# The gate projection as a Strassen-Winograd product: three of its seven quarter products between the attention's matmuls, four in a stage behind the pooling projection

## The chip, the cores and the metric

The kernel runs on one core of a Trainium2 chip. The metric is device time in microseconds (us) of one execution, from the first to the last instruction with what the launch adds around it; of the kernel before, three executions are given, and one more was taken with a profile.

## The reference, cut to what matters

One residual layer on 1024 tokens with 1024 channels, in fp32. What the change touches is the line with `gates`; what stands around it decides where that work may be placed.

```
h = rmsnorm(x, g_mix)
z = h @ w_in                       # pooling | q | k | v columns
y_pool = pool_mixer(u_pool, w_pool_grp, pool_scale)
y_attn = diff_attention(q, k, v, g_q, g_k, lam, g_sub)     # 8 heads
gates  = sigmoid(h @ w_gate + b_gate)                      # 1024 x 2048
merged = gates[:, :1024] * (y_pool @ w_branch_pool)
       + gates[:, 1024:] * (y_attn @ w_branch_attn)
x = x + merged @ w_out
x = x + square(relu(rmsnorm(x, g_ffn) @ w_up)) @ w_down
```

The matrix h enters as its transpose hT (channels by tokens), and so every gate block is 128 gate columns by 1024 tokens.

## The kernel before, in words

**Arithmetic.** Every fp32 operand of a matmul is split into a high part (a cast, made by ScalarE) and a low part (source minus high part, made by VectorE or GpSimd; `split`, L115). A product is then three matmuls into one PSUM bank, high by high, high by low, low by high (`mm3`, L120; its three calls are L123, L124 and L125, and after the change L122, L123 and L124). "A matmul of 512 columns" below is one of those three.

**Stages.** First come the norm of x and its transpose into hT (8 tiles of four 128-channel blocks each in high and low parts). Then the attention: 8 heads with 8 query tiles each, a software pipeline whose stages run one or more tiles apart (`stage_qkv` makes z for tile t, `stage_prep` norms it, `stage_qkT` transposes q and k (tk), `stage_scores` (sc), `stage_aT` transposes the weights (ta), `stage_pv` (po), `stage_norm`). Names such as z5_6 mean head 5, tile 6. z has two PSUM banks, sc two, the transposes (tk, ta) two, po one, and one bank is left for the fillers (`ps_f`, tag "f").

**Fillers.** Two kinds of independent matmuls are written behind the attention in the program, and so have a lower priority: the pooling mixer (u, 24 matmuls for each of 8 pieces, and yp, 3 each) and the gate projection (`gate_cols`, L744: 16 column blocks, each 2 halves of 24 matmuls, named g0 to g15; the result plus bias goes through a two-buffer pool "fo" to the DRAM tensor `g_dram`). The order on each engine is fixed when the program is built: a list scheduler takes, at each step, the instruction of highest priority whose inputs it expects to be ready. A filler therefore stands wherever it expected TensorE to have nothing of the attention to do; what is left of them runs behind the attention. Each engine, and each queue of transfers (SyncE's "SP" and ScalarE's), works strictly in the order given.

**Behind the attention.** The pooling projection bp (`branch_pool`, L218; 16 groups of 12 matmuls; the result stays in SBUF as mp), then the attention's projection ba (16 groups of 24), multiplied by the gates that are read back from `g_dram` (`gate`, L207, which applies the sigmoid), then the output projection op, then the MLP. The MLP's two projections are already Strassen-Winograd products before the change.

**Scheme.** With hT and w_gate cut in halves each way (channels by tokens, gate columns by channels), the 2 by 2 block product needs 8 quarter products the plain way, and 7 by Winograd's form of Strassen's scheme with sums of quarters as operands. For each of 8 column blocks d (128 columns of the first and the same 128 of the second gate half), one quarter product is 4 blocks of k by three matmuls: 12 matmuls of 512 columns.

Of the kernel before, what the change touches and what calls it, by code (L numbers as in the profile page):

```python
# [17 lines left out]
P = 128  # L18
S = 1024
# [18 lines left out]
N_QKVW = 8 * H  # L38
# [11 lines left out]
G_FIRST, G_Z = 13, 13  # L50
# [5 lines left out]
def encoder_kernel(  # L56
# [63 lines left out]
    def mm3(ps, lhs_hi, lhs_lo, rhs_hi, rhs_lo, first, last, more=False):  # L120

        kw = {"skip_group_check": True} if more else {}  # L122
        nc.tensor.matmul(ps, lhs_hi, rhs_hi, start=first, stop=False, **kw)  # L123
        nc.tensor.matmul(ps, lhs_hi, rhs_lo, start=False, stop=False, **kw)  # L124
        nc.tensor.matmul(ps, lhs_lo, rhs_hi, start=False, stop=last, **kw)  # L125

    wcount = [0]

    def wt(shape, name, dt=F32R):

        wcount[0] += 1
        if wcount[0] > N_QKVW and (wcount[0] - N_QKVW - 1) % (N_W + N_FW) >= N_W:
            return fw_tile(shape, name, dt)
# [73 lines left out]
    def gate(gts, c):  # L207
        for gt, c0, c1 in gts:
            nc.sync.dma_start(gt, g_dram[c * P : (c + 1) * P, c0:c1])
            nc.scalar.activation(gt, gt, AF.Sigmoid, bias=zero)  # L210

    def whole(g):
        return [(g, 0, S)], [g[:, 0:512], g[:, 512:S]]
# [3 lines left out]

    def branch_pool(d, ws, ps_fn):  # L218

        m = htile([P, S], F32, f"mp{d}", 1)  # L220
        for th in range(2):
            ps = proj_T(ps_fn(f"bp{d}_{th}"), ws, lambda k, th: pair(ypT[k][th]), th, nk=4)
            nc.scalar.copy(m[:, th * 512 : (th + 1) * 512], ps)
        mp.append(m)
# [14 lines left out]
    zero = const.tile([P, 1], F32, name="zero")  # L239
    y_dram = dram.tile([D, S], F32, name="y_dram")  # L240
# [48 lines left out]
    with ExitStack() as ph:  # L289
# [119 lines left out]
        gghs = {}  # L409
# [19 lines left out]
        def stage_qkv(h, t):  # L429
# [4 lines left out]
            for k in range(NK):  # L434
# [3 lines left out]
                mm3(z[:, 0:384], l_hi, l_lo, w[:, 0, :], w[:, 1, :], k == 0, k == NK - 1)  # L438
# [47 lines left out]
        def stage_scores(h, t):  # L486
# [44 lines left out]
            if (h, t) == (H - 1, NT - 1):  # L531

                nc.vector.tensor_scalar(zero, Z[:, 1, t : t + 1], 0.0, None, op0=ALU.mult)
            st[h, t]["a"] = s[0]
# [209 lines left out]
    def gate_cols(c):  # L744
        ws = fill_w(w_gate, c * P, f"gate{c}")
        for th in range(2):
            ps = fill_proj(ws, th, f"g{c}_{th}", spare_bank if c >= G_Z else fill_bank)
            fo = fo_tile(f"go{c}_{th}")
            nc.scalar.activation(fo[:, 0:512], ps, AF.Identity, bias=cols[:, c : c + 1])  # L749
            nc.scalar.dma_start(g_dram[c * P : (c + 1) * P, th * 512 : (th + 1) * 512], fo[:, 0:512])  # L750
            yield

    def gates():
        for c in range(2 * NK - 2):
            yield from gate_cols(c)
        for gen in [gate_cols(c) for c in (2 * NK - 2, 2 * NK - 1)] * 2:
            next(gen)
            yield

    gate_units = gates()  # L760
    for _ in range(G_FIRST):
        next(gate_units)
    for g in range(4):
        for _ in pool_group(g):
            next(gate_units)
    for _ in gate_units:
        pass
# [16 lines left out]
    def ypt_tile(shape, dt, name, th):  # L784
        return htile(shape, dt, name, 0)
# [10 lines left out]


    ws_bp = {0: load_cols2(w_branch_pool, 0, "bp0")}
    ypT = [load_split(p_dram, g * P, f"ypT{g}", ypt_tile) for g in range(4)]
    mp, yT, ws_ba = [], [], {}  # L800

    for d in range(NK):
        if d % 2 == 0 and d + 2 < NK:
            ws_bp[d + 2] = load_cols2(w_branch_pool, (d + 2) * P, f"bp{d + 2}")
        elif d > NK - 4:
            j = len(ws_ba)
            ws_ba[j] = load_cols(w_branch_attn, j * P, f"ba{j}")
        branch_pool(d, ws_bp[d - d % 2][d % 2], bank)
        if d % 4 < 2:
            rb = [fu_tile(f"rb{d}") if d % 2 else ut([P, S], F32, f"rb{d}")]  # L810
        else:
            rb = [tmp(f"rb{d}_{i}") for i in range(2)]
        yT.append(load_split(y_dram, d * P, f"yT{d}", yt_tile(d), (rb, r_dram[d])))
    mT = {}
    for d in range(NK):
# [3 lines left out]
        gp = [tmp(f"gp{d}_{th}") for th in range(2)]  # L819
        gate([(gp[0], 0, 512), (gp[1], 512, S)], d)  # L820
        for th in range(2):
# [506 lines left out]
```

## Time and profile before

| | us |
|---|---|
| three executions | 1574.85, 1574.85, 1577.69 |
| median | 1574.85 |
| the profiled execution: its time / its span | 1577.1 / 1575.3 |
| busy in the span: TensorE matmul / VectorE / ScalarE / GpSimd | 1549.7 / 936.4 / 814.5 / 356.0 |

The span runs from the first to the last instruction; 1.8 us of the profiled execution's time lie around it. The busy time of TensorE overstates its work, since a matmul of 512 columns is shown with 0.39 us while the next one starts 0.23 us after it; so it is the starts, or the number of matmuls in a stretch, that tell how dense TensorE is. By the rows' times, attention runs from about 25 us to 629 us (its last z at 576), the rest of the fillers to 722, bp to 765, ba to 855, op and the second norm to about 950, and the MLP to the end.

### The profile page before, as it was taken

The page shows a single profiled execution, that of the slowest core. Times are in us where ns is not written, and L with a number is a line of the kernel's source. Part 1 is how long each engine was busy: PE and PEld are TensorE (multiplying, and loading weights), DVE is VectorE, ACT ScalarE, POOL GpSimd, SP SyncE. Part 2 cuts the span into 40 slices and gives each one's busy share as a digit, 9 for nine tenths or more (in the row PEclk, how much of TensorE's full clock was granted, in tenths as well). Part 3 has the DMA queues.
Part 4 walks back from the last instruction along what each step waited for, and adds up shares of the span by engine and source line. Part 5 has one row for each costly group of instructions (what it writes and reads, how often), then busy time and mean ns, then how long its engine had stood idle before and what let it go on. Part 6 is the DMA issues. An engine that isn't in the chain of part 4 may idle for free.

```text
span 1575.3 us, 21905 instructions
## 1 busy us (share of the span) xinstructions
PE 1549.7 (98%) x7713; PEld 1328.0 (84%) x7713; DVE 936.4 (59%) x1925; ACT 814.5 (52%) x1810; POOL 356.0 (23%) x456
## 2 busy tenths in 40 slices
PE   7999999999999999899999999999999999999999
PEld 6999999999999997688888887888888788888887
DVE  6766666666676766206442358866655667546562
ACT  6656575765656665225542547555555633333331
POOL 5424252433434332313454400000000000000000
PEclk9999999999999999999999999999999999999999
DMA  7102020201112112229547533554342799437650
GB/s 226 56 29 75 28 71 26 69 29 55 58 36 64 45 53 76 91 100 309 159 128 219 172 114 122 185 185 157 128 140 107 274 345 355 161 121 253 221 186 27
DMA packets 168008, 206.94 MB, mean 131 GB/s; under 512 B 10117, under 2 KB 104026, under 8 KB 167898
## 3 DMA queue, kind: packets, MB, share of 16 engines
q1 hardware_dynamic: 150490, 178.23, 34.8%
q10 hardware_dynamic: 17408, 27.30, 4.7%
q8 instruction: 61, 1.00, 0.3%
q14 instruction: 49, 0.40, 0.1%
HBM read 150.94 MB, written 54.56 MB: 130 GB/s over the span
## 4 chain that ended last, share of the span: by engine, by line
PE 91%; DMA 3%; ACT 2%; DVE 2%; issue 1%; SPq 0%; POOL 0%; ACTq 0%; DVEq 0%; POOLq 0%
PE z L125 5%; PE z L123 5%; PE z L124 5%; PE Da L124 4%; PE Da L123 4%; PE g L123 4%; PE Da L125 4%; PE g L124 4%; PE g L125 4%; PE Db L124 3%; PE Db L123 3%; PE Db L125 3%; PE X L125 2%; PE X L123 2%; PE X L124 2%; PE sc L508 2%
## 5 line engine op out<-in xcount | busy, mean ns | idle before, releaser
L125 PE MATMUL z<-wqkv,hT 128*128 128x384 f32 x512 | 174.6, 341 | 0.3 <-DVE hT L118 0.2
L123 PE MATMUL z<-wqkv,hT 128*128 128x384 f32 x512 | 174.6, 342 | 0.1
L124 PE MATMUL z<-wqkv,hT 128*128 128x384 f32 x512 | 174.0, 340 | 0.0
L519 ACT ACTIVATE s<-s,nm 128x256 f32<-128x256 f32 (+7 forms) x128 | 99.7, 779 | 57.7 <-DVE nm L511 56.2
L123 PE MATMUL g<-hT,fwgate 128*128 128x512 f32 x256 | 101.7, 398 | 4.5 <-ACT go L749 2.4
L449 POOL TENSOR_TENSOR ms<-ms,mhalf 128x4 f32<-128x4 f32 x64 | 70.7, 1104 | 156.0 <-DVE ms L447 153.2
L124 PE MATMUL g<-hT,fwgate 128*128 128x512 f32 x256 | 101.6, 397 | 0.0
L125 PE MATMUL g<-hT,fwgate 128*128 128x512 f32 x256 | 100.8, 395 | 0.0
L123 PEld LDWEIGHTS z<-wqkv,hT 128*128 128x128 f32 x512 | 96.9, 189 | 3.7 <-ACT hT L117 0.7
L125 PEld LDWEIGHTS z<-wqkv,hT 128*128 128x128 f32 x512 | 96.8, 189 | 3.1 <-DVE hT L118 1.4
L124 PEld LDWEIGHTS z<-wqkv,hT 128*128 128x128 f32 x512 | 96.9, 189 | 2.9
L511 DVE CUSTOM_DVE_ANT_0 s<-sc,dist 128x512 f32<-128x512 f32 (+3 forms) x128 | 74.9, 587 | 23.0 <-PE sc L509 21.5
L508 PE MATMUL sc<-K,Q 128*128 128x512 f32 (+2 forms) x192 | 69.0, 362 | 0.7 <-DVE nm L511 0.5
L509 PE MATMUL sc<-K,Q 128*128 128x512 f32 (+2 forms) x192 | 66.5, 355 | 0.0
L118 DVE TENSOR_TENSOR AS<-s,AS 128x512 fp32r<-128x512 f32 x64 | 43.9, 690 | 35.4 <-ACT AS L117 35.2
L118 POOL TENSOR_TENSOR wqkv<-rqkv,wqkv 128x384 fp32r<-128x384 f32 x60 | 62.4, 1058 | 7.9 <-ACT wqkv L117 6.7
L123 PEld LDWEIGHTS g<-hT,fwgate 128*128 128x128 f32 x256 | 48.4, 189 | 15.3 <-ACT go L749 3.9
L118 POOL TENSOR_TENSOR fwgate<-frgate,fwgate 128x512 fp32r<-128x512 f32 x32 | 42.9, 1343 | 72.0 <-ACT fwgate L117 72.0
L125 PEld LDWEIGHTS g<-hT,fwgate 128*128 128x128 f32 x256 | 48.5, 190 | 9.0
L458 POOL TENSOR_TENSOR qn<-qn,ggh 128x128 f32<-128x128 f32 x64 | 30.1, 470 | 115.0 <-DVE qn L452 101.9
L479 DVE TENSOR_TENSOR K<-tk,K 64x128 fp32r<-64x128 f32 x128 | 36.9, 288 | 31.9 <-ACT K L478 28.2
L124 PEld LDWEIGHTS g<-hT,fwgate 128*128 128x128 f32 x256 | 48.5, 189 | 8.1
(424 smaller groups left out, 4548.8 us busy)
## 6 DMA issues: line engine op xcount, KB each, us to landing
wd<-in_w_down_dram SPq DMA_DIRECT2D x56, 512.0 KB, 5.2
wu<-in_w_up_dram SPq DMA_DIRECT2D x32, 512.0 KB, 5.5
udS<-us SPq DMA_DIRECT2D x64, 256.0 KB, 2.4
ur<-udS SPq DMA_DIRECT2D x32, 512.0 KB, 4.8
rqkv<-in_w_in_dram SPq DMA_DIRECT2D x64, 192.0 KB, 2.8
ud<-u ACTq DMA_DIRECT2D x48, 256.0 KB, 2.5
ur<-ud SPq DMA_DIRECT2D x24, 512.0 KB, 3.8
frgate<-in_w_gate_dram SPq DMA_DIRECT2D x32, 256.0 KB, 2.7
```

The source lines that it names most:

```text
L118: return (lo_eng or nc.vector).tensor_tensor(lo, src, f(hi), op=ALU.subtract)
L123: nc.tensor.matmul(ps, lhs_hi, rhs_hi, start=first, stop=False, **kw)
L124: nc.tensor.matmul(ps, lhs_hi, rhs_lo, start=False, stop=False, **kw)
L125: nc.tensor.matmul(ps, lhs_lo, rhs_hi, start=False, stop=last, **kw)
L449: nc.gpsimd.tensor_tensor(ms, ms, mhalf[:, 0:4], op=ALU.pow)
L458: nc.gpsimd.tensor_tensor(qn[:, 2:4, :], qn[:, 2:4, :], ggh.unsqueeze(1).broadcast_to([P, 2, HD]), op=ALU.mult)
L479: nc.vector.tensor_tensor(K[other, m, c0 : c0 + P], k, f(k_hi), op=ALU.subtract)
L508: nc.tensor.matmul(dst, Q[:, i, 0, :], rhs, start=True, stop=False)
L509: nc.tensor.matmul(dst, Q[:, i, 1, :], rhs, start=False, stop=True)
L511: nc.vector.tensor_tensor_reduce(out=s[i][:, c : c + w], in0=sc[:, 0:w], in1=dist[:, o0 + c : o0 + c + w], scale=2.0 ** -(h + 1), scalar=B ...
L519: nc.scalar.activation(s[i][:, 0:n], s[i][:, 0:n], AF.Exp, bias=last, scale=-1.0, accum_out=Z[:, i, t : t + 1])
```

## The change

The 16 plain column blocks (8 by 2 by 2 by 24, 768 matmuls of 512 columns) are replaced by 8 blocks d of 7 quarter products (672 matmuls).

- **As fillers** (`gate_first`): products A11*B11 and A12*B21 into one bank (gA), and S4*B22 into another (gB). After the first product ScalarE copies the bank out (x1, to the new DRAM tensor `xz`), and the second product accumulates onto it, which gives the finished quarter C11. The operand S4 = A11 + A12 - A21 - A22 is made on GpSimd from four loads of a weight quarter; these loads share a pool of two buffers ("fr"). `G_TAIL = 5`: only the blocks 0 to 2 are free to go anywhere; 3 to 7 are held back with `issue_after` until the third-last z of the last head.
- **In a stage of their own** (`gate_rest`), behind the pooling projection: first the quarters of hT are replaced in place by T2, T1, T3 and T4 (16 additions and subtractions of 128x1024, ten on VectorE and six on GpSimd, and 8 splits), then for each d the four products with S2, S1, S3, A22. VectorE splits these operands and adds the PSUM results to x1 and z3 read back from `xz`; finished quarters go to `g_dram`.
- The loads and the splitting of the attention's result (`load_yT`) move from the pooling projection into this stage. The pooling projection's result goes out to DRAM (`mp_dram`) and comes back in ba. The gate's bias is added in the sigmoid (`gbias`).

```diff
-G_FIRST, G_Z = 13, 13
+G_FIRST, G_Z, G_TAIL = 4, 3, 5
...
-            nc.scalar.activation(gt, gt, AF.Sigmoid, bias=zero)
+            nc.scalar.activation(gt, gt, AF.Sigmoid, bias=gbias[:, c : c + 1])
...
+    def gate_first(d):
+        rows_d = slice(d * P, (d + 1) * P)
+        r11, r12 = gate_raw(11, d), gate_raw(12, d)
+        w11, w12 = gate_split(r11, f"A11_{d}"), gate_split(r12, f"A12_{d}")
+        ps = spare_bank(f"gA{d}") if d >= G_Z else fill_bank(f"gA{d}")
+        mm_quarter(ps, w11, 0, 0, True, True)
+        keep(ps, xz[rows_d, 0, :], f"x1_{d}")
+        nc.gpsimd.tensor_tensor(r12, r11, r12, op=ALU.add)
+        mm_quarter(ps, w12, 2, 0, False, True, True)
+        keep(ps, g_dram[rows_d, 0:512], f"C11_{d}")
+        for q in (21, 22):
+            nc.gpsimd.tensor_tensor(r12, r12, gate_raw(q, d), op=ALU.subtract)
+        w4 = gate_split(r12, f"S4_{d}")
+        yield
+        ps = spare_bank(f"gB{d}") if d >= G_Z else fill_bank(f"gB{d}")
+        mm_quarter(ps, w4, 2, 1, True, True)
+        keep(ps, xz[rows_d, 1, :], f"z3_{d}")
+        yield
...
+    early, late = units[: 2 * (NK - G_TAIL)], units[2 * (NK - G_TAIL) :]
...
+    with tc.issue_after(z_last[H - 1, NT - 1 - 2].ins):
+        for gen in late:
+            next(gen)
...
+    for kp in range(2):
+        a, b, c, e = (fw_tile([P, 2, 512], f"comb{n}{kp}", F32) for n in "abce")
...
+        add(dve, a, f(B12[0]), f(B12[1]))
+        add(pool, b, f(B22[0]), f(B22[1]))
+        add(pool, e, f(B21[0]), f(B21[1]))
+        sub(dve, c, b, a)
+        sub(dve, a, a, f(B11[0]))
+        sub(dve, a, a, f(B11[1]))
+        sub(dve, b, b, a)
+        sub(pool, e, e, b)
+        for room, t in ((B11, b), (B12, a), (B22, c), (B21, e)):
+            split(*room, t)
...
+        for name, rw in (("S2", r11), ("S1", s1), ("S3", r21), ("A22", r22)):
+            w = wt([P, 2, 4, P], f"{name}_{d}")
+            split_made[d] = split(w[:, 0], w[:, 1], rw)
...
+        A = bank(f"gA_{d}")
+        gate_mm(A, ws[0], 2, True, True)
+        add(dve, u[:, 0, :], A, v[:, 0, :])
```

Two places where the order of instructions moves. The first is TensorE in head 5, at the end of z5_5. Before the change, gate matmuls (g6_1) stand between the scores of the tile (sc5_1):

```order
L125 MATMUL z5_5_4639<-wqkv5_7_3987,hT3_1_1_339 128x384
L123 MATMUL g6_1_7174<-hT0_1_0_332,fwgate6_0_7087 128x512
L124 MATMUL g6_1_7174<-hT0_1_1_333,fwgate6_0_7087 128x512
L125 MATMUL g6_1_7174<-hT0_1_0_332,fwgate6_0_7087 128x512
L509 MATMUL sc5_1_0_0_4526<-K5_0_4156,Q2_238 128x256
L123 MATMUL g6_1_7174<-hT0_1_0_332,fwgate6_0_7087 128x512
```

After it, at the same place on TensorE, the rows are those of the attention alone:

```order
L124 MATMUL z5_5_4640<-wqkv5_7_3988,hT3_1_1_340 128x384
L491 MATMUL sc5_1_0_0_4527<-K5_0_4157,Q2_239 128x256
L548 MATMUL ta4_7_0_4455<-identf_90,s4_7_0_4330 128x128 x4
L492 MATMUL sc5_1_0_0_4527<-K5_0_4157,Q2_239 128x256
L491 MATMUL sc5_1_1_0_4550<-K5_0_4157,Q2_239 128x256
L548 MATMUL ta4_7_1_4475<-identf_90,s4_7_0_4330 128x128 x4
```

In the changed order no filler stands between the last yp behind z4_5 and the first gA4 behind z7_5, which is 24 tiles (z4_6 to z7_5); before, there were 11 to 26 fillers at the tiles 0, 1 and 5 of these heads.

The second place is GpSimd in the drain of the attention, between qn7_7 (the normed q and k of the last tile) and the memsets of the last two weight tiles (AT7_2, AT7_3). Before the change:

```order
L458 TENSOR_TENSOR qn7_7_6425<-qn7_7_6425,ggh7_5720 128x128
L118 TENSOR_TENSOR wgrp2_7469<-rgrp2_7467,wgrp2_7469 128x128
L551 MEMSET AT7_2_4_6450 128x128 x2
L722 COPY sum2_0_1_7499<-u2_7472 128x1
L722 COPY sum2_0_2_7502<-sum2_0_1_7499 128x2
L722 COPY sum2_0_4_7505<-sum2_0_2_7502 128x4
```

After it the operands of the held-back blocks stand there (A11_5 and A12_5 are splits of loaded quarters, ga12_5 the sum that becomes S4_5):

```order
L117 TENSOR_TENSOR S4_4_7436<-ga12_4_7390,S4_4_7436 128x512
L441 TENSOR_TENSOR qn7_7_6426<-qn7_7_6426,ggh7_5721 128x128
L117 TENSOR_TENSOR A11_5_7459<-ga11_5_7455,A11_5_7459 128x512
L117 TENSOR_TENSOR A12_5_7462<-ga12_5_7457,A12_5_7462 128x512
L765 TENSOR_TENSOR ga12_5_7457<-ga11_5_7455,ga12_5_7457 128x512
L535 MEMSET AT7_2_4_6451 128x128 x2
L769 TENSOR_TENSOR ga12_5_7457<-ga12_5_7457,ga21_5_7497 128x512
L769 TENSOR_TENSOR ga12_5_7457<-ga12_5_7457,ga22_5_7500 128x512
L117 TENSOR_TENSOR S4_5_7503<-ga12_5_7457,S4_5_7503 128x512
```

The chain of these operands is now in one queue with the attention's own small operations.

More of the change, by code (lines that the diff above doesn't have):

```diff
@@ L753, in gates, with gate_raw @@
[L753 to L760, printed above, removed]
+    xz = dram.tile([D, 2, 512], F32, name="xz")
+    def gate_raw(q, d):
+        r0, c0 = (q % 10 - 1) * 512, (q // 10 - 1) * D + d * P
+        rw = fr_tile([P, 4, P], f"ga{q}_{d}")
+        nc.sync.dma_start(rw, w_gate[r0 : r0 + 512, c0 : c0 + P].rearrange("(kk p) c -> p kk c", p=P))
+        return rw
@@ L802, in encoder_kernel @@
+    gens = [gate_rest(d) for d in range(NK)]
     for d in range(NK):
```

170 lines of the change are left out of this document (119 added, 51 removed).

## The prediction

> **What bounds the kernel now.** I read the page first (busy shares, the chain that ended last), then TensorE by windows, then its starts where the windows thin out.
>
> ```profile
> PE 1549.7 (98%) x7713; PEld 1328.0 (84%) x7713; DVE 936.4 (59%) x1925; ACT 814.5 (52%) x1810; POOL 356.0 (23%) x456
> ...
> PE 91%; DMA 3%; ACT 2%; DVE 2%; issue 1%; SPq 0%; POOL 0%; ACTq 0%; DVEq 0%; POOLq 0%
> ```
>
> The chain of waits is TensorE for 91%, so a matmul less is time less, as long as nothing else becomes late. The price of one is not its 0.39 us but the distance between starts. A window inside ba, where only matmuls of 512 columns run (time, TensorE busy and count, clock, share of the transfer engines, GB/s):
>
> ```profile
> 775.00:800.00 25.00, 25.00 (x108) 1.00 0.46 149
> ```
>
> 25 / 108 = **0.2315 us** each. In the attention the same view gives, for 480 us, all engines (TensorE, weight loads, VectorE, ScalarE, GpSimd), then TensorE alone for z, g, u and yp in this order:
>
> ```profile
> 80.00:560.00 480.00, 479.46 (x2893) 449.63 (x2892) 322.69 (x977) 300.06 (x890) 180.22 (x251) 1.00 0.16 48
> 80.00:560.00 480.00, 264.55 (x1277) 1.00 0.16 48
> 80.00:560.00 480.00, 87.51 (x326) 1.00 0.16 48
> 80.00:560.00 480.00, 25.62 (x96) 1.00 0.16 48
> 80.00:560.00 480.00, 2.85 (x9) 1.00 0.16 48
> ```
>
> 1277 / 24 = 53.2 tiles, 9.02 us each. The 431 fillers cost 431 x 0.2315 = 99.8 us of that; the attention by itself asks TensorE for (480 - 99.8) / 53.2 = **7.15 us** a tile. TensorE never stands still here, but it is full because there are fillers, which is the point on which this prediction turns.
>
> **The change part by part.** *Fewer matmuls.* 768 become 672: 96 x 0.2315 = **-22.2 us**. The order of the changed program on TensorE has 672 rows of gA and gB where 768 of g stood, so the change does what it says.
>
> *The thin stretch behind the attention goes.* All engines, then the starts at one place in it:
>
> ```profile
> 629.40:722.00 92.60, 86.19 (x366) 68.56 (x365) 17.30 (x27) 27.20 (x46) 27.36 (x26) 0.98 0.37 121
> ```
>
> ```profile
> 650.62 0.39 PE L125 MATMUL g<-hT,fwgate 128*128 128x512 f32 x1
> 651.84 0.50 PE L123 MATMUL yp<-mix,wgrp 128*128 128x512 f32 x1 [0.83 <-ACT go L749]
> ...
> 654.48 0.63 PE L125 MATMUL g<-hT,fwgate 128*128 128x512 f32 x1
> 654.91 0.63 PE L123 MATMUL g<-hT,fwgate 128*128 128x512 f32 x1
> ```
>
> 366 matmuls ask for 84.7 us and took 92.6: 7.9 us are lost, because the fillers of one bank wait for ScalarE to empty it. In the changed order these fillers are gone from here, and bp with 8 banks follows the attention: **-7.9 us**. What is late next is the drain of the attention, below.
>
> *The heads without fillers.* In 24 tiles no filler is left. If TensorE stays the bound, a tile takes 7.15 us; if the other engines need the 9.02 us that they have now, the fillers were free and nothing is won: the bounds are 0 and 24 x 1.87 = +44.9 us against the sum. In between lies what VectorE needs of its own, 322.7 / 53.2 = 6.07 us a tile, and the waits in which ScalarE has to act first and that no faster TensorE removes, in the same window (busy, mean ns, then the idle time before them and its releaser):
>
> ```profile
> L479 DVE TENSOR_TENSOR K<-tk,K 64x128 fp32r<-64x128 f32 x105 | 30.3, 289 | 29.1 <-ACT K L478 26.4
> L481 DVE TENSOR_TENSOR Q<-tk,Q 64x128 fp32r<-64x128 f32 x104 | 29.8, 286 | 13.9 <-ACT Q L480 12.0
> L118 DVE TENSOR_TENSOR AT_0l<-ta,AT_0h 128x512 fp32r<-128x512 f32 x35 | 24.2, 690 | 15.0 <-ACT AT_0h L117 14.0 <-ACT oq L588 0.7
> ...
> L526 DVE RECIPROCAL cf<-Z 128x1 f32<-128x1 f32 x54 | 8.8, 162 | 27.4 <-ACT s L519 27.0
> ```
>
> 26.4 + 12.0 + 14.0 + 27.0 = 79.4 us, 1.49 a tile. 6.07 + 1.49 = 7.56 us: just above TensorE's 7.15. I take 7.56, **+9.8 us** (24 x 0.41), since it is the only value that rests on waits and not on an extreme.
>
> *The drain of the attention.* The five held-back blocks start behind z7_5 (557.7 in the trace). The stretch from there to the last po, all engines, then g, u and yp:
>
> ```profile
> 557.70:629.40 71.70, 69.83 (x390) 60.10 (x389) 46.58 (x127) 41.15 (x115) 19.39 (x29) 1.00 0.21 66
> 557.70:629.40 71.70, 18.83 (x72) 1.00 0.21 66
> 557.70:629.40 71.70, 18.29 (x72) 1.00 0.21 66
> 557.70:629.40 71.70, 2.66 (x9) 1.00 0.21 66
> ```
>
> Without its 153 fillers (35.4 us) the drain is 36.3 us; with 180 new ones 78.0, which the sum of matmuls contains. But their operands come one after another through two load buffers. The steps, from the nearest rows: a cast, a low part, an addition, a load.
>
> ```profile
> L117 ACT CAST fwgate<-frgate 128x512 fp32r<-128x512 f32 x12 | 7.4, 619 | 20.8 <-PE g L125 17.5 <-PE u L125 3.1 <-DMA frgate<-in_w_gate_dram 0.2
> ```
>
> ```profile
> L831 POOL TENSOR_TENSOR mg<-mg,mp 128x512 f32<-128x512 f32 x16 | 21.5, 1343 | 25.2 <-DVE mg L830 25.2
> L118 POOL TENSOR_TENSOR fwgate<-frgate,fwgate 128x512 fp32r<-128x512 f32 x14 | 18.3, 1310 | 47.9 <-ACT fwgate L117 47.9
> ```
>
> ```profile
> frgate<-in_w_gate_dram SPq DMA_DIRECT2D x32, 256.0 KB, 2.7
> ```
>
> One block: 3 additions (4.03), 3 loads in line (8.1), 2 casts (1.24), 2 low parts (2.62) = 16.0 us. Four such rounds are 64 us of a stretch of 78, so 14 us remain for queueing: what waits behind these steps is GpSimd's own memsets and qn7_7, and behind gB6 and gA7 on TensorE the last ta and po. At best nothing is lost. At worst each of the 10 steps finds one other GpSimd instruction ahead (180.22 / 251 = 0.72 us in the attention): 7.2 us a round, 28.7 in all, of which 15 stick out. I take a value near the low end, since the 14 us of room come first: **+4 us**.
>
> *The stage of its own.* Per block TensorE has 48 matmuls, 11.1 us. VectorE has 4 low parts, 2 scalings and 2 low parts for yT, 4 additions from PSUM. Their rows, and transfers beside bp today:
>
> ```profile
> L823 DVE TENSOR_TENSOR mp<-mp,gp 128x512 f32<-128x512 f32 x16 | 16.2, 1022 | 21.3 <-ACT gp L210 21.1
> L118 DVE TENSOR_TENSOR yT<-ryT,yT 128x512 fp32r<-128x512 f32 x16 | 14.8, 971 | 3.9 <-ACT yT L117 3.9
> ...
> L830 DVE TENSOR_TENSOR mg<-ba,ga 128x512 f32<-128x512 f32 x16 | 10.9, 684 | 0.4 <-PE ba L125 0.4
> ```
>
> ```profile
> 722.00:765.00 43.00, 43.00 (x191) 35.53 (x190) 27.75 (x28) 27.56 (x49) 19.11 (x14) 1.00 0.83 271
> ```
>
> At 0.684 throughout, 12 operations are 8.2 us; with 0.97 for the eight that read SBUF twice, 10.5. Both fit under 11.1. GpSimd's four additions are 5.4 us. The loads and stores are about 3 MB a block, 276 GB/s: what bp bears today (271 GB/s at 0.83) with TensorE full. Bounds: nothing, and, if VectorE and GpSimd could never overlap, 8.2 + 5.4 - 11.1 = 2.5 us a block, +20 us. I take a quarter of it, as the 10.5 still leave 0.6 us a block: **+5 us**.
>
> The shorter VectorE durations belong to operations from PSUM, the longer to those with two SBUF inputs beside a busy GpSimd. The Trainium skill, "SBUF — State Buffer", section "Who interferes with whom", calls this an exclusive lock: one of the two engines blocks for the whole instruction. The rows agree in direction (1.02 against 0.68); by the rule taken strictly the stage would cost the +20 and not the +5, the third rival.
>
> *At nothing:* rebuilding hT. An operation of 1024 columns on VectorE:
>
> ```profile
> L118 DVE TENSOR_TENSOR u_0l<-ur,u_0h 128x1024 fp32r<-128x1024 f32 x1 | 1.2, 1227 | 0.4 <-ACT u_0h L117 0.4
> ```
>
> 18 of them are 22 us, and GpSimd's six, at twice 1.343, 16; both lie beside bp's 192 matmuls (44 us), and without that cover they are +22. The pooling result's way through DRAM costs two stores per 5.6 us and one load per 11.1 in stages whose transfers have room (0.46 in ba).
>
> **Sum:** -22.2 - 7.9 + 9.8 + 4 + 5 = -11.3. The profiled execution took 1577.1, so 1565.8; the median lies 2.25 below it: **1563.5 us**.
>
> **The rivals.**
> - *Nothing waits:* -30.1, 1545. For it: in all 480 us TensorE shows no wait, so every other engine keeps up with it today. Against it: VectorE's 7.56, and two queues with a chain of loads behind z7_5.
> - *The fillers were free:* the heads keep up to 9.02 us a tile, since they stand just where the scheduler saw a gap. At 9.02 the sum is +23.8, 1599. It decides from 7.56 + 11.3 / 24 = 8.03 us a tile; from there the change is slower. For it: VectorE and ScalarE together have 622.8 us of work in 480, so they seldom rest at once. Against it: each is idle for a third of the time, and VectorE's 7.56.
> - *VectorE and GpSimd exclude each other* in the new stage: +20 for +5, 1578.5.
> - *The slow clock.* Behind two waits of 1 us, at 651 and 653, the granted clock fell to half:
>
> ```profile
> 654.00:656.00 2.00, 2.00 (x6) 1.55 (x5) 0.00 (x0) 0.00 (x0) 0.00 (x0) 0.50 0.38 139
> ```
>
> Eight matmuls at 0.43 in place of 0.23 lost 1.6 us. If every place where a block of fillers stood in these tiles (about five a head, 14 in all) does this, +22: 1586. The Trainium skill, "TensorE: Matmul & The Clock Gate", Part 1, wants an idle window of about 3.4 us for it; by that, holes of 1 us would cost nothing, and the trace here shows that two of them sufficed.
>
> **How the numbers follow.** Forecast 0.52 (1552 to 1572), nothing waits 0.12, free fillers 0.18, exclusion 0.12, clock 0.06. The range reaches from 1547, just above the first rival, to 1586 with the clock, and leaves out the worst of the second. A difference of 0.2%, 3.1 us, is about what a measurement of this kernel can tell. Faster by more: forecast 0.50 and first rival, 0.62; within: edges of the forecast and of the exclusion, 0.11; slower: free fillers, half of the exclusion, most of the clock, 0.27.
>
> **What will show it.** Tiles z4_6 to z7_5 at 7.6 us (7.15 and 9.0 are the rivals); no window with waits on ScalarE for a bank behind the attention; fewer than 5 us of TensorE waiting at gB6, gA7, gB7 for S4 and A12; in the new stage about 108 matmuls per 25 us. Wrong would be a longer attention, or a stage in which TensorE waits for VectorE's low parts.

## The result, and the profile after

The changed kernel takes **1611.83 us** (median of 4 executions, 1610.63 to 1616.73), the kernel before beside it 1576.27 (4 executions, 1574.85 to 1579.47). The ratio is 1.0229, with a 95% interval of 1.0201 to 1.0256: 2.3% slower, where 1563.5 us was forecast. The profiled execution is the longest of the four (1616.7 us, its span 1614.9), so the sums below, made between the two profiled executions (1577.1 and 1616.7), explain +39.6 us, four more than the medians differ.

The page of the changed kernel:

```profile
PE 1558.2 (96%) x7617; PEld 1324.0 (82%) x7617; DVE 1019.7 (63%) x2004; ACT 820.1 (51%) x1824; POOL 443.6 (27%) x508
...
PE 41%; DMA 2%; DVE 1%; ACT 0%; issue 0%; POOL 0%; SPq 0%; ACTq 0%; DVEq 0%
```

TensorE executes 96 matmuls less and is busy 8.5 us longer. The second line is cut short by what the profile could follow back; that TensorE has 41% where it had 91% is no measure of waiting. For that the work is cut into the same four stages in both kernels: first z to last z, from there to the end of bp (with the thin stretch or the drain's fillers), then to the first op, then the rest. Windows before (columns: length, then busy time and count of TensorE, weight loads, VectorE, ScalarE and GpSimd, granted clock, share of the transfer engines, GB/s), and after:

```profile
11.00:575.60 564.60, 563.62 (x3370) 527.02 (x3371) 383.79 (x1158) 360.07 (x1072) 225.62 (x310) 1.00 0.18 57
575.60:761.50 185.90, 177.61 (x817) 144.51 (x816) 79.36 (x141) 82.22 (x164) 56.72 (x56) 0.99 0.43 140
761.50:851.10 89.60, 89.60 (x385) 72.09 (x385) 34.36 (x44) 36.83 (x57) 45.79 (x34) 1.00 0.46 145
851.10:1575.30 724.20, 716.89 (x3137) 582.73 (x3135) 436.26 (x578) 331.51 (x510) 23.02 (x23) 1.00 0.54 184
```

```profile
10.80:571.80 561.00, 543.61 (x3200) 503.40 (x3200) 396.47 (x1176) 352.85 (x1068) 245.84 (x334) 0.98 0.19 60
571.80:690.40 118.60, 108.49 (x509) 87.48 (x507) 75.51 (x113) 59.58 (x129) 69.45 (x48) 0.97 0.50 162
690.40:888.20 197.80, 185.61 (x769) 148.20 (x770) 106.80 (x131) 69.64 (x106) 95.42 (x67) 0.96 0.61 198
888.20:1614.90 726.70, 718.69 (x3137) 583.32 (x3135) 438.21 (x581) 334.11 (x515) 28.14 (x27) 1.00 0.55 185
```

From each stretch its matmuls of 512 columns are taken off at 0.2315 us. Up to the last z these are 503 fillers before and 336 after; then 481 fillers and 192 of bp before, 168 and 192 after; then 384 of ba before, and 384 of the four products and 384 of ba after. What is left is the attention's own work, and waiting:

| stretch | before | after | difference | the prediction's terms |
|---|---|---|---|---|
| first z to last z | 564.6 - 116.4 = 448.2 | 561.0 - 77.8 = 483.2 | **+35.0** | +9.8 |
| to the end of bp | 185.9 - 155.8 = 30.1 | 118.6 - 83.3 = 35.3 | **+5.2** | -7.9 + 4 |
| own stage and ba | 89.6 - 88.9 = 0.7 | 197.8 - 177.8 = 20.0 | **+19.3** | +5 |
| start, op and MLP | | | +2.3 | 0 |
| 96 matmuls fewer | | | -22.2 | -22.2 |
| sum | | | **+39.6** | -11.3 |

So the saving came as forecast, and 61.8 us were lost around it. The attention has 167 fillers less (38.7 us) and became 3.6 us shorter. The clock column shows a second thing. It falls to 0.5 for 3.4 us at a time, in ten places, 40.9 us together; before it did so once. Three of them:

```profile
44.60:48.00 3.40, 3.40 (x10) 2.62 (x9) 1.31 (x5) 1.25 (x4) 2.88 (x3) 0.50 0.21 80
362.00:365.40 3.40, 3.40 (x16) 3.19 (x15) 2.63 (x9) 1.65 (x7) 1.01 (x1) 0.50 0.41 145
713.60:720.40 6.80, 5.71 (x13) 4.46 (x14) 6.80 (x8) 1.10 (x3) 3.69 (x3) 0.50 0.34 110
```

Three holes in front of TensorE, each with the rows that lead to it (start, us, engine, line, operation, in brackets the idle time before and its releaser). At the start, GpSimd's `rs` of a token norm stands behind an addition for S4 that waited for its load, and VectorE's `hn` waits for `rs`:

```profile
38.56 1.29 POOL L769 TENSOR_TENSOR ga<-ga,ga 128x512 f32<-128x512 f32 x1 [1.54 <-DMA ga<-in_w_gate_dram]
39.81 0.55 POOL L232 TENSOR_TENSOR rs<-rs,mhalf 128x1 f32<-128x1 f32 x1
40.39 2.42 DVE L253 SCALAR_TENSOR_TENSOR hn<-x,rs,gmb 128x512 f32<-128x512 f32 x2 [1.29 <-POOL rs L232]
43.29 0.63 PE L258 MATMUL hps<-identf,hn 128*128 128x128 f32 x4 [2.94 <-DVE hT L117]
```

In the new stage, the sum s1 waits 8.2 us for a buffer that a store of bp's result still holds (both go through "fo"), and S2 is made from s1. Its cast also stands on ScalarE behind a copy of bp's result (mp) that waits 5.6 us for the same buffers; both waits end within 0.2 us of each other:

```profile
697.87 1.29 POOL L821 TENSOR_TENSOR s<-gr 128x512 f32<-128x512 f32 x1 [8.22 <-DMA mp_dram<-mp]
701.45 0.59 ACT L755 COPY mp<-bp 128x512 f32<-128x512 f32 x1 [5.56 <-DMA mp_dram<-mp]
702.43 0.62 ACT L116 CAST S<-ga 128x512 fp32r<-128x512 f32 x1 [0.40 <-ACT mp L755]
703.10 0.61 PE L122 MATMUL gA<-hT,S 128*128 128x512 f32 x1 [4.02 <-ACT S L116]
```

And in bp, a copy that would free a PSUM bank stands on ScalarE behind a cast that waits 4.5 us for a load:

```profile
647.60 1.14 ACT L116 CAST wbp<-rbp 128x512 fp32r<-128x512 f32 x2 [4.45 <-DMA rbp<-in_w_branch_pool_dram]
648.64 0.58 ACT L755 COPY z<-gB 128x512 f32<-128x512 f32 x1
649.27 0.79 PE L122 MATMUL bp<-ypT,wbp 128*128 128x512 f32 x1 [3.20 <-ACT z L755]
```

### The profile page after: what moved, and what is told of

The parts are those of the page before. It is cut to its first block, busy times and chain, and to the rows that moved or that the text cites. A ratio compares the mean times of both kernels' runs of the same rounds, so it can differ in the third digit from the quotient of the medians.

```text
span 1614.9 us, 21978 instructions
## 1 busy us (share of the span) xinstructions
PE 1558.2 (96%) x7617; PEld 1324.0 (82%) x7617; DVE 1019.7 (63%) x2004; ACT 820.1 (51%) x1824; POOL 443.6 (27%) x508
## 5 line engine op out<-in xcount | busy, mean ns | idle before, releaser
L548 PE MATMUL ta<-identf,s 128*128 128x128 f32 x288 | 48.2, 277 | 7.0 <-DVE s L511 3.4
L465 ACT CAST Q<-tk 64x128 fp32r<-64x128 f32 x128 | 33.2, 260 | 39.6 <-DVE Q L464 37.0
L122 PE MATMUL op<-wo,mT 128*128 128x512 f32 x128 | 50.2, 395 | 1.8 <-ACT wo L116 1.8
L463 ACT CAST Q<-tk 64x128 fp32r<-64x128 f32 x128 | 33.0, 258 | 36.7 <-DVE K L462 35.4
L124 PE MATMUL ba<-yT,wba 128*128 128x512 f32 x128 | 50.5, 395 | 0.0
L122 PE MATMUL ba<-yT,wba 128*128 128x512 f32 x128 | 50.5, 395 | 0.0
L123 PE MATMUL ba<-yT,wba 128*128 128x512 f32 x128 | 50.5, 395 | 0.0
```

Source lines behind the costliest of these rows:

```text
L124: return nc.tensor.matmul(ps, lhs_lo, rhs_hi, start=False, stop=last, **kw)
L465: nc.scalar.copy(Q[other, m, 1, :], q)
L548: nc.tensor.transpose(ta[:, i * P : (i + 1) * P], a[:, (4 * j + i) * P : (4 * j + i + 1) * P], identf)
```

## The experiments

The theory from these rows: the loss has two parts, the place of the work (the attention lacks fillers) and single instructions that stand in an engine's strict queue behind something that waits; both make holes, and holes bring the half clock. The times of single executions vary by 2 to 5 us, so differences below that are read from traces.

**e1: no block held back.**

```diff
-G_FIRST, G_Z, G_TAIL = 4, 3, 5
+G_FIRST, G_Z, G_TAIL = 4, 8, 0
```

> The changed kernel, but none of the eight blocks of first products is held back (G_TAIL 0, all of them in the fillers' bank). By its order on TensorE all 504 fillers then stand between z0_0 and z6_5: heads 5 and 6 get 150 and head 7 and the drain none, where the changed kernel has none in heads 5 to 7 and 168 in the drain. Theory 1 (without fillers a tile needs 8.1 us because its own steps wait for one another, with fillers 9.0): heads 5 and 6 go from 65 to about 72 us each, head 7 stays near 63, and the drain falls from 68 us to about 48, since 39 us of matmuls leave it and not all of its holes can close; 1600 to 1610 us in all. Rival (a tile without fillers is TensorE's 7.15 us, and what the changed kernel lost there was the half clock behind its holes): heads 5 and 6 at 75 us, head 7 at 58 us, drain 37 us, about 1590.

Measured 1612.2 us (one execution), 2 us above theory 1's range. With 78 and 72 fillers the heads 5 and 6 took 75.0 and 80.5 us, where theory 1 had 72 for each and the rival 75; head 7 without any took 63.3, as theory 1 had it, and the drain without any 57.3 us, nine more than the theory gave it. The drain's window:

```profile
594.90:652.20 57.30, 40.03 (x178) 28.82 (x176) 47.00 (x103) 32.83 (x81) 10.34 (x12) 0.73 0.21 68
```

A clock of 0.73 over 57 us: 30.7 us of it ran at half. The rival's 1590 is out, though its 75 us was right for head 5, and the theory had the drain too cheap. The lack of fillers only moved from heads 5 and 6 to head 7 and the drain.

**e3: the old products in the new places.** Plain blocks, two of them free and 14 held back:

```diff
-    for _ in range(G_FIRST):
+    for _ in range(4):
         next(gate_units)
     for g in range(4):
         for _ in pool_group(g):
-            next(gate_units)
-    for _ in gate_units:
-        pass
+            pass
+    with tc.issue_after(z_last[H - 1, NT - 1 - 2].ins):
+        for _ in gate_units:
+            pass
```

> The kernel before with its plain gate blocks, but only two of them are free fillers beside the pooling mixer; the other 14 are held back until the third-last z, as the change holds its five blocks. In its order the heads 5 to 7 have 13 fillers instead of 205. No Strassen product in the gates at all: this is the place of the work alone. Theory 1 (fillers cost a tile 0.9 us where they fill 2.06): heads 5 to 7 at 8.1 us a tile, 65 us each instead of 73, and the time rises by about 180 x 0.2315 less some 20, with the thin one-bank stretch longer: +20 to +38 us, 1597 to 1615. Rival (TensorE bound, 7.15 to 7.56 us a tile): 0 to +12, 1577 to 1589.

Measured 1592.9 us, **+16.2** against 1576.7 beside it, with no Strassen product in the gates at all. It lies between the two expectations, and so does the tile: head 6, with no filler, took 60.7 us, 7.59 a tile, not 8.1. Heads 5 (13 fillers) and 6:

```profile
362.90:426.80 63.90, 62.71 (x384) 58.10 (x383) 49.39 (x148) 41.74 (x131) 25.94 (x37) 1.00 0.15 46
426.80:487.50 60.70, 59.04 (x371) 55.53 (x370) 45.96 (x145) 40.41 (x131) 23.19 (x36) 1.00 0.12 36
```

The same heads of the changed kernel, both with no filler, at 8.21 and 8.07 us a tile and a clock of 0.97:

```profile
378.70:444.40 65.70, 61.39 (x372) 56.96 (x371) 45.77 (x146) 40.60 (x131) 24.24 (x39) 0.97 0.11 33
444.40:508.90 64.50, 61.03 (x370) 57.05 (x369) 46.15 (x146) 41.26 (x131) 22.47 (x35) 0.97 0.14 42
```

Each of these heads has one stretch of half clock, at most 1.7 us of its time or 0.2 a tile. The attention's own time per tile, head duration less fillers at 0.2315 us, over 8:

| head | 0 | 1 | 2 | 3 | 4 | 5 | 6 | 7 |
|---|---|---|---|---|---|---|---|---|
| before | 6.16 | 7.08 | 7.21 | 7.12 | 7.11 | 7.12 | 7.11 | 7.12 |
| changed | 6.82 | 7.08 | 7.14 | 7.32 | 8.25 | 8.21 | 8.07 | 7.52 |
| e3, plain, held back | 6.13 | 7.08 | 7.36 | 7.26 | 7.54 | 7.60 | 7.59 | 7.47 |
| e6 (below) | 6.99 | 7.08 | 7.14 | 7.32 | 8.16 | 7.96 | 7.60 | 7.42 |
| e12, mixed (below) | 6.24 | 7.13 | 7.18 | 7.18 | 7.21 | 7.18 | 7.27 | 7.11 |

Of the 35.0 us, some 16 go with the place alone (e3's whole row is 16.0 above before's). It may be more, since e3 still has 51 fillers in heads 5 to 7 and the changed kernel 12.

The price of a filler can be read here too. Head 6 of the kernel before, with 68 fillers:

```profile
430.70:503.40 72.70, 72.70 (x438) 68.23 (x437) 49.67 (x152) 45.41 (x138) 27.04 (x39) 1.00 0.15 47
```

72.7 less e3's 60.7 is 12.0 us for 68 fillers, 0.18 each, both at full clock.

**e4: fillers that do nothing.**

```diff
+    wd = gate_split(gate_raw(11, 0), "wd")
+    for i in range(14):
+        mm_quarter(fill_bank(f"dm{i}"), wd, 0, 0, True, True)
```

> The changed kernel with 168 more fillers that nobody reads (14 groups of 12 matmuls of 512 columns on a first weight quarter), which by the order fall into heads 4 to 7: 69, 60 and 39 in heads 5, 6 and 7. It does extra work and leaves nothing out. At full price they are 38.9 us. Theory 1 (other engines' steps set the pace of a tile without fillers): a tile goes from 8.1 to 9.0 us, half the price or less, +10 to +20 us; the half-clock stretches in the heads go. Rival (a tile is TensorE's 7.15 and the rest is the half clock): the fillers cost their full price less the clock's 2 to 4 us, +35. Third (fillers are entirely free): within 4 us of the changed kernel's 1612.

Measured 1625.3 us, +13.5 against the changed kernel's median. Heads 5 and 6:

```profile
376.60:449.60 73.00, 73.00 (x440) 68.41 (x440) 46.13 (x144) 42.13 (x130) 22.53 (x35) 1.00 0.09 27
449.60:520.60 71.00, 71.00 (x431) 66.64 (x430) 46.65 (x144) 42.04 (x129) 23.42 (x36) 1.00 0.13 39
```

69 and 60 fillers lengthened them by 7.3 and 6.5 us: **0.11 us for a filler that costs 0.2315 elsewhere**. The clock is at 1.00 and TensorE without a gap again; part of the low price is the half clock that went with the fillers' return, at most 1.7 us a head. Less its fillers at full price, head 5 is back at 7.13 us a tile, where the kernel before has 7.12. Theory 1 holds; neither "full price" nor "free".

**e2: buffers of its own for bp's result.**

```diff
+        mo = ut([P, S], F32, f"mo{d}")
...
-            keep(ps, mp_dram[d * P : (d + 1) * P, hs], f"mp{d}_{th}")
+            nc.scalar.copy(mo[:, hs], ps)
+            nc.scalar.dma_start(mp_dram[d * P : (d + 1) * P, hs], mo[:, hs])
```

> The changed kernel, but the pooling projection's result goes to DRAM through buffers of its own (three of the class U, a whole row block each) instead of the two buffers fo, which the operand sum s1 of the last four products also uses. Theory 1 (the own stage starts late because s1 of blocks 0 and 1 waits behind stores of the pooling projection for a buffer fo): the waits of gA for ScalarE's casts at 699 and 710 us and the half clock behind them go, -6 to -12 us, 1600 to 1606. Rival (VectorE and GpSimd block one another there, and the operands come late for that): the work of both is the same, so no more than -2 us.

Measured 1602.5 us, -9.4. From the end of bp to op it took 187.6 us (687.7 to 875.3) in place of 198.6 (689.6 to 888.2): -11.0. The waits for S at 699 and 710 us are gone, one of 2.7 us for `uv` took their place. So more than half of what the own stage lost hung on one shared buffer class.

**e5: the first S4 behind the token norms**, on top of e2:

```diff
+            z_last[h, t, "qn"] = nc.gpsimd.tensor_tensor(
...
-        nc.gpsimd.tensor_tensor(r12, r11, r12, op=ALU.add)
...
+        with tc.issue_after(z_last[0, 2, "qn"].ins) if d < 2 else ExitStack():
+            nc.gpsimd.tensor_tensor(r12, r11, r12, op=ALU.add)
+            for q in (21, 22):
+                nc.gpsimd.tensor_tensor(r12, r12, gate_raw(q, d), op=ALU.subtract)
```

> The kernel with the buffers of their own for the pooling projection's result (1602.5 us), and in it the three additions that make S4 of blocks 0 and 1 stand on GpSimd behind qn0_2, so behind the last of the token norms' small operations (rs5 to rs7), not between them. Theory 1 (at 40 us TensorE waits 2.9 us because rs6 stood on GpSimd behind an addition that waited for its load, and VectorE's hn ran beside GpSimd at 1.2 us in place of 0.7; then comes 3.4 us of half clock): head 0 falls from 68.5 us to about 61 with 18 fillers fewer, which heads 4 and 5 take up at less than half price; 1596 to 1600. Rival (the hole belongs to the start itself, and the S4 operations merely lie in it): within 1.5 us of 1602.5.

Measured 1595.2 us, -7.3. The window that held the start's hole, in the changed kernel and in this one:

```profile
25.00:50.00 25.00, 22.01 (x121) 19.35 (x120) 18.34 (x44) 14.70 (x40) 18.33 (x17) 0.93 0.30 99
```

```profile
25.00:50.00 25.00, 24.73 (x149) 22.65 (x148) 18.51 (x58) 16.30 (x51) 12.29 (x14) 1.00 0.16 57
```

28 matmuls more in the same 25 us. Where six additions stand in the queue of an engine that is 27% busy was worth some 7 us, because an instruction of 0.55 us stood behind them.

**e6: S4 of the held-back blocks on VectorE**, on top of e2:

```diff
+        eng = nc.vector if d >= 3 else nc.gpsimd
-        nc.gpsimd.tensor_tensor(r12, r11, r12, op=ALU.add)
+        eng.tensor_tensor(r12, r11, r12, op=ALU.add)
```

> The kernel with the buffers of their own for the pooling projection's result (1602.5 us), and in it the additions that make S4 of the held-back blocks 3 to 7 run on VectorE in place of GpSimd (15 operations, 20 us off GpSimd's queue). Theory 1 (the drain's holes, 9 us, and 10 us of half clock behind them come from the chain of operands in GpSimd's queue): the last po comes 5 us earlier, 1595 to 1599. Rival (the drain waits for the attention's own last steps and for loads, whoever adds): within 2 us.

Measured 1609.4 us, 6.9 slower than e2, beyond both expectations: the theory on the drain is not borne out. The last po came at 637.6 us as in e2. And a new hole of 20 us opened in bp, in front of one transposition (trr) whose operand r7 goes through GpSimd. GpSimd and TensorE there:

```profile
661.51 3.12 POOL L822 TENSOR_TENSOR combe<-hT,hT 128x1024 f32<-128x1024 f32 x1
664.59 2.24 POOL L822 TENSOR_TENSOR s<-gr 128x512 f32<-128x512 f32 x1
666.80 2.25 POOL L825 TENSOR_TENSOR gr<-ga,gr 128x512 f32<-128x512 f32 x1
669.01 1.18 POOL L597 TENSOR_TENSOR r<-r,rz 128x8 f32<-128x8 f32 x1
670.24 0.37 PE L599 MATMUL trr<-identf,r 128*8 128x128 f32 x1 [19.66 <-POOL r L597]
```

What bounds the drain of the changed kernel stays open: in e6 it holds 344 matmuls and in e2 313, since bp begins earlier, so the two last po tell little.

The run shows something else. Its head 6 executes the instructions of e3's head 6 in the same order on every engine, and takes the same time, with no filler and at full clock:

```profile
442.90:503.60 60.70, 58.99 (x370) 55.59 (x369) 45.91 (x145) 40.62 (x130) 23.11 (x35) 1.00 0.15 44
```

The changed kernel and e2 execute the same instructions there in another order, and take 64.5 and 64.0 us. So of the changed kernel's head 6, 3.8 us hang on the order that the list scheduler gave the attention itself, at most 1.7 of them by the half clock; no Strassen operand is made in that head.

**e8: no GpSimd additions in the rebuilding of hT and the own stage**, on top of e2:

```diff
-    dve, pool = nc.vector, nc.gpsimd
+    dve, pool = nc.vector, nc.vector
```

> The kernel with the buffers of their own for the pooling projection's result (1602.5 us), and in it the additions of the rebuilt hT and of the own stage that GpSimd made (6 of 1024 columns and 32 of 512) run on VectorE. Theory 1 (the two engines exclude each other, so that GpSimd's 1.3 to 1.7 us for an addition is lost to VectorE, which needs 0.7): VectorE's low parts beside it fall from about 1.0 to 0.7 us, the waits for uv in the own stage shrink, -2 to -5 us. Rival (GpSimd's share is a real help): VectorE has 16 operations a block, 11 us beside TensorE's 11.1, and becomes the bound, +3 to +12 us.

Measured 1598.7 us, -3.8, at the edge of what one execution tells. The durations tell more. VectorE's low parts of S beside GpSimd's additions (e2), and without these (e8), 690 to 830 us:

```profile
L117 DVE TENSOR_TENSOR S<-gr,S 128x512 fp32r<-128x512 f32 x6 | 7.8, 1306 | 0.0
L117 DVE TENSOR_TENSOR S<-s,S 128x512 fp32r<-128x512 f32 x6 | 7.5, 1252 | 0.0
```

```profile
L117 DVE TENSOR_TENSOR S<-gr,S 128x512 fp32r<-128x512 f32 x6 | 4.1, 687 | 0.4 <-ACT S L116 0.4
L117 DVE TENSOR_TENSOR S<-s,S 128x512 fp32r<-128x512 f32 x6 | 4.1, 685 | 0.0
```

0.69 us alone, 1.25 to 1.31 beside GpSimd, whose addition VectorE makes in 0.69: handing these to GpSimd gains nothing here.

**e10: the three remedies together**, on top of e5, which holds e2's:

```diff
-    dve, pool = nc.vector, nc.gpsimd
+    dve, pool = nc.vector, nc.vector
```

> All eight blocks with seven products and five of them held back, with the three remedies together: own buffers for the pooling projection's result, the early S4 behind the token norms, no GpSimd additions in the rebuilding and in the own stage. If the three causes are separate, their gains add: 1595.2 - 3.8 = 1591.4 us, within 3; what then remains above the kernel before, 15 us, is the place of the work. If they share one cause (one late engine), less than that: 1594 to 1598.

Measured 1590.9 us (one execution), against 1591.4 by the sum: they add, so within what such a time tells the causes are separate. The 15 us that remain above the kernel before look like e3's 16, and the expectation took them for it, but that is a coincidence. e3 executes all 768 gate matmuls, and this kernel saves 22.2 us of them, so some 36 us are still lost against the profiled execution before. By the same four stages: +27.5 to the last z, -0.4 to the end of bp, +5.0 in the own stage with ba, +3.9 at the start and from op on. The first of them:

```profile
10.90:564.40 553.50, 536.03 (x3203) 498.74 (x3202) 397.47 (x1176) 352.62 (x1068) 244.60 (x334) 0.99 0.20 61
```

553.5 less 336 fillers (77.8) is 475.7 us of own time in the attention, 11.5 more than e3's 464.2. The remedies leave this part open.

**e7: three plain blocks, five with seven products**, on top of e2. The fillers come back: 522 between the first and the last z.

```diff
+    DS = [1, 2, 3, 4, 5]
+    early = [gen for c in (0, NK) for gen in [gate_cols(c, fill_bank)] * 2]
+    early += [gen for gen in map(gate_first, DS) for _ in range(2)]
+    late = [gen for c in (6, 6 + NK, 7, 7 + NK) for gen in [gate_cols(c, spare_bank if c >= 7 else fill_bank)] * 2]
...
-    gens = [gate_rest(d) for d in range(NK)]
+    gens = [gate_rest(d) for d in DS]
+    LY = [[0], [1, 2], [3, 4], [5, 6], [7]]
```

> Blocks 0, 6 and 7 of the gates are plain column blocks again (96 matmuls each, all fillers), blocks 1 to 5 keep the seven products, none is held back, and the pooling projection's result has its own buffers; the loads of the attention's result are spread over five blocks of the own stage. 708 matmuls in place of 672 or 768. By its order the heads 0 to 7 have 53, 75, 65, 65, 76, 80, 52 and about 56 fillers, the drain some 160: as many as in the kernel before. Theory 1 (what the change lost in the attention is the fillers that it took from there): -13.9 for 60 fewer matmuls, -7.9 for the thin stretch, +8 for the own stage, about 1563 us, 1558 to 1570. Rival (the seven products cost by their operands, wherever they stand): 8 to 15 us of holes remain in the heads and the drain as well, 1572 to 1580.

Measured 1582.4 us, a miss by 19 and beyond the rival too. The attention behaved (its own time 451.9 us, 3.7 above before's), but bp stood twice, for 6.3 and 5.3 us, for its second weights, with 13.6 us of half clock. The rebuilding of hT, written ahead of these weights, held ScalarE's queue: its cast waited for a GpSimd addition that took 7.28 us while VectorE worked beside it.

```profile
643.41 7.28 POOL L832 TENSOR_TENSOR combe<-combe,combb 128x1024 f32<-128x1024 f32 x1 [8.00 <-DVE combb L832]
650.72 1.04 ACT L116 CAST hT<-combe 128x1024 fp32r<-128x1024 f32 x1 [4.59 <-POOL combe L832]
654.85 0.80 PE L122 MATMUL bp<-ypT,wbp 128*128 128x512 f32 x1 [6.30 <-ACT wbp L116]
```

**e9: the rebuilding on VectorE alone and behind the splits of ypT.** Its code moves into bp's loop:

```diff
-            split(t[:, 0, :], t[:, 1, :], rw[:, th * 512 : (th + 1) * 512])
+            last_lo[0] = split(t[:, 0, :], t[:, 1, :], rw[:, th * 512 : (th + 1) * 512])
...
+        if d == 0:
+            with tc.issue_after(last_lo[0].ins):
+                for kp in range(2):
...
+                    add(dve, b, f(B22[0]), f(B22[1]))
+                    add(dve, e, f(B21[0]), f(B21[1]))
```

> The mixed kernel (three plain blocks, five with seven products; 1582.4 us), and in it the rebuilding of hT stands on VectorE alone and behind the splits of the pooling mixer's result, in place of between them. In the mixed kernel TensorE waited 6.5 and 5.7 us at 648 and 657 us for the second weights of the pooling projection, whose buffer came free late, with 13.7 us of half clock after. Theory 1 (the rebuilding, in the queues of ScalarE, VectorE and GpSimd ahead of these splits, made them late): both waits and their clock go, -12 to -18 us, 1564 to 1571, faster than the kernel before. Rival (the weights come late for their load's place in SyncE's queue): no more than -4, 1578 to 1583; and VectorE, now alone with 30 us of rebuilding, may make the own stage late by some us.

Measured 1577.5 us, 1.0014 of the kernel before (95% interval 1.0004 to 1.0024). That is 4.9 us less than e7's one execution, where the theory gave 12 to 18 and the rival at most 4. Half of the theory held: the waits for the weights fell to 0.8 and 1.0 us, but trr stood 5.3 us for r7, whose small operations were now queued behind the rebuilding.

**e11: r7 ahead of the rebuilding on VectorE, and ahead of bp4's low parts on GpSimd.**

```diff
-            with tc.issue_after(last_lo[0].ins):
+            with tc.issue_after(last_lo[0].ins), tc.issue_after(last_r[0].ins):
...
+            with tc.issue_after(last_r[1].ins) if d else ExitStack():
-            ws_bp[d + 2] = load_cols2(w_branch_pool, (d + 2) * P, f"bp{d + 2}")
+                ws_bp[d + 2] = load_cols2(w_branch_pool, (d + 2) * P, f"bp{d + 2}")
```

> The mixed kernel with the rebuilding on VectorE (1577.5 us), and in it the three small operations of the last head's reciprocal (r7) stand on VectorE ahead of the rebuilding, and the low parts of the pooling projection's later weights (bp4, bp6) stand on GpSimd behind r7's. In the kernel before this one TensorE stood 5.3 us at 660 us in front of one transposition (trr) that waits for r7, and 6.8 us of half clock followed. Theory 1 (the queue's order alone): the wait falls below 1 us and the clock stays up, -6 to -9 us, 1568 to 1572, 0.3% faster than the kernel before. Rival (something else is late there, the load of the weights for bp4): no more than -3.

The wait in front of trr fell from 5.3 to 2.9 us, not below 1. The profiled execution took 1572.9 us, but the median of ten is 1576.5, ratio 1.0004 (0.9993 to 1.0015): by the median it changed nothing. Its executions spread over 5.8 us, and why is open.

**e12: e11 with the loads of the attention's result later.**

```diff
-    LY = [[0], [1, 2], [3, 4], [5, 6], [7]]
+    LY = [[0], [1], [2, 3], [4, 5], [6, 7]]
```

> The same with the loads of the attention's result spread later over the five blocks of the own stage: one, one, two, two and two in place of one, two, two, two and one. Theory 1 (the wait of 2.5 us for VectorE's low part of S at 733 us, and its 3.4 us of half clock, come from two loads' worth of VectorE work in the second and third block): -2 to -4 against its sibling. Rival (the work is only moved, and the attention's projection waits for the last two loads instead): +1 to +4.

Measured **1567.4 us** (median of 4, 1566.6 to 1571.7), ratio **0.9945** (0.9928 to 0.9961): faster than both kernels, at 60 of the 96 saved matmuls. Between the medians of the siblings lie 9.1 us, more than the theory gave; between their profiled executions (1572.9 and 1571.7) only 1.2, so the trace does not show where they come from. The wait for the low part of S is gone from e12's own stage, but one of 3.1 us for `uv` stands there with 6.8 us of half clock, and the stage is 1.3 us longer than e11's. Its attention and its stage to the end of bp, against the windows at the top:

```profile
10.90:583.30 572.40, 569.76 (x3391) 532.11 (x3390) 398.09 (x1183) 370.61 (x1097) 262.72 (x348) 1.00 0.22 69
583.30:691.40 108.10, 103.78 (x497) 85.56 (x497) 73.86 (x117) 54.58 (x115) 38.43 (x25) 0.97 0.42 140
```

572.4 less 522 fillers (120.8) is 451.6 us of own time, where the changed kernel has 483.2 and the kernel before 448.2. With the fillers back (and the start free of the early S4), 31.6 of the 35.0 us in the attention are gone.

## Why the prediction was wrong, step by step

- **Fewer matmuls, -22.2:** right; the pitch is unchanged (109 per 25 us in ba).
- **The heads without fillers, +9.8, is the step that failed most.** Its tile of 7.56 us was met in number by e3's head 6, 7.59 at full clock, but in part by luck: VectorE was busy 5.7 us a tile there and not 6.07 (the window of the prediction holds VectorE's work for the fillers too), and its waits on ScalarE in the four groups of the sum were 0.64 us and not 1.49, together 6.4. That these waits set the pace is not shown. The step failed in four ways. The sum counted only tiles without any filler, but e3 lost 5.8 us in heads 2 to 4 as well, where the fillers were merely fewer or fell at other places. It held the clock at 1.00, and five stretches of half clock in heads 0 to 6 took up to 1.7 us each, 8.5. It had nothing for the start, where a 2.9 us wait came with the first S4. And it took the order of the attention's own instructions as given, which cost at least 2 us in head 6 (e6). 16 + 8.5 + 2.9 leave at least 7.6 of the 35.0 us, and the order is part of that rest; how large a part in the other heads is open, and so are the 11.5 us that e10 still loses beyond e3.
- **The free fillers, as a rival:** 9.02 us a tile did not happen (8.2 and 8.07), but the break-even of 8.03 that the prediction gave was passed. By e4 a filler costs 0.11 us there, less than half its price. The prediction saw that "it is full because there are fillers" and then priced their departure at 9.02 - 7.56 = 1.46 us for some 8 fillers a tile, 0.18 each. That is what e3 gives for a head without half clock; in the changed kernel it was 0.11.
- **The thin stretch and the drain, -7.9 + 4:** +5.2 in place of -3.9. The thin stretch went, and the waits of 2.8 us before 627 and of 3.2 before 649 us, each with 3.4 us of half clock, replaced it. The chain through two buffers, named as the reason, is not shown: e6 moved its additions and the last po came no earlier, and the two drains hold different work.
- **The own stage, +5:** +19.3. The bill of VectorE's durations was not the main limit. e2 shows 11.0 us of it as the waits of s1 and of bp's copies for the buffers that bp's stores held; nothing in the sum had asked which pool an operand's tile comes from. VectorE and GpSimd do slow one another (e8), but taking GpSimd's additions away gained 3.8 us, not 20.
- **The rebuilding "at nothing":** its time was hidden beside bp in the changed kernel. Its place in the queues was not harmless: in e7, e9 and e6 TensorE waited 5 to 20 us through one cast or one small operation behind it.
- **The slow clock as a rival (+22, chance 0.06):** ten stretches, 40.9 us at half, up to 20 us. That holes bring it was right. That the size came near 22 is luck: the forecast had 14 places in the heads without fillers, and two stretches lie there. The mistake was to count it as an alternative; it follows holes, whatever makes them, so it belongs to each of the other cases as a surcharge.
- **What was to be shown:** tiles at 7.6 (8.1), no wait for a bank behind the attention (3.2 us at 649), under 5 us for S4 and A12 (1.7 at 598 and 0.6 at 619, right), 108 matmuls per 25 us in the own stage (60 at 700, 83 at 775, wrong).

## What to carry to other kernels

Count the fillers as a stock: the attention and its drain had 656 places for them (503 and 153), and where these were left empty a filler taken away won 0.11 us in the changed kernel and 0.18 in e3, not its 0.2315, so a saving in matmuls must be reckoned at what their place was worth. A remainder that equals another run's loss is no proof of the same cause: compare the two stage by stage, with the saving put back. For every instruction that a change adds, write down what stands behind it in its strict queue and which buffer class its tile shares: the three remedies were worth 4 to 11 us each, on engines that are 27 to 63% busy. And reckon that some 2 us of holes within 3.4 can cost up to 1.7 us more, for the half clock behind them.

## What the runs showed of the hardware

**The clock's windows.** In the changed kernel the granted clock fell ten times, and each time at a multiple of 3.413 us from the others (44.6, 324.5, 362.0, 385.9, 464.4, 628.3, 648.7, 703.3, 713.6, 778.4 us), for 3.4 or 6.8 us. I took the distances between the starts of its matmuls, less the usual pitch, as holes, and added them up in windows of that grid. Up to 1000 us, the windows at full clock that were followed by half clock had 1.8 to 3.2 us of holes out of 3.41, and those not followed by it at most 1.8; the last tenth depends on what is taken as the usual pitch. Several waits below 1 us add up: some 2.2 us of holes before 362.0 came from waits of 0.2 to 0.5 us. The one stretch in the kernel before (653.8) fits, with 2.0 us. So the limit lies near half a window, but the sum of the holes alone does not settle it. In e5 a window with 2.05 us of holes was not followed by half clock, and one with 1.5 to 1.7 us was (each window, then the one behind it):

```profile
628.40:631.80 3.40, 1.51 (x7) 0.90 (x5) 3.33 (x3) 0.67 (x2) 3.40 (x3) 1.00 0.42 139
631.80:635.20 3.40, 3.13 (x14) 2.56 (x15) 0.69 (x2) 1.96 (x4) 3.40 (x4) 1.00 0.58 198
304.10:307.50 3.40, 2.12 (x12) 1.55 (x11) 2.00 (x7) 3.06 (x10) 0.83 (x2) 1.00 0.12 39
307.50:310.90 3.40, 3.40 (x9) 2.61 (x8) 2.50 (x10) 1.69 (x6) 0.46 (x1) 0.50 0.21 80
```

The Trainium skill, "TensorE: Matmul & The Clock Gate", Part 1, gives the free-running window of 3413 ns, which these runs show, and an idle window as the condition, where here a window about half idle sufficed.

**VectorE beside GpSimd.** A low part of 128x512 with both inputs in SBUF took VectorE 0.69 us alone and 1.25 to 1.31 beside GpSimd's additions, and GpSimd's 128x1024 addition took 7.28 us while VectorE had one operation after the other (e7); the same operation took 3.38 at its other place in that trace. The Trainium skill, "SBUF — State Buffer", "Who interferes with whom", says that either may block, by the order of issue; the rows show both directions, and do not tell whether the order of issue decides.
